# A decoder layer on one core: gate sums by distance, gates turned by transposes, the running maximum broadcast from 128 rows, and one turned output moved behind the next head's values

## The chip, the cores and the metric

The kernel runs on one core of a Trainium2 chip. A core has five engines with queues of their own. TensorE (PE in the profile; its weight loads are PEld) multiplies matrices, VectorE (DVE) and ScalarE (ACT) work element by element, GpSimd (POOL) does more of that, and SyncE (SP) issues DMAs. [...] The metric is the device time of one execution in microseconds, here the median of three runs.

## The reference

One layer of a decoder trunk for 512 positions of 1024 channels, in float32. A mixer comes first, then a feed-forward part with a short convolution; only the mixer's first group is touched by the change. It is an mLSTM with four heads of 256, worked in chunks of 128 positions:

```python
b = jnp.cumsum(lf_, axis=-1)              # lf_: log of the forget gate
dmat = jnp.where(causal, b[..., :, None] - b[..., None, :] + i_[..., None, :], -jnp.inf)
m_t = jnp.maximum(b + m[..., None], jnp.max(dmat, axis=-1))
scores = jnp.einsum("bhtd,bhsd->bhts", q_, k_) * jnp.exp(dmat - m_t[..., None])
h = num / jnp.maximum(jnp.abs(den), jnp.exp(-m_t))[..., None]
```

`num` and `den` carry a state from chunk to chunk. Each head's `h` is then normalised over its 256 channels, multiplied by a gain and by a sigmoid, and goes with the result of a convolution group (31 taps) into one output projection.

## The kernel before

**Matmuls.** The large products are made in three float32r passes: each operand is split into a high and a low part (`w_split` on ScalarE and GpSimd for weights), and `mm3` (lines 198 to 202) adds high x high, high x low and low x high. A projection of 128 columns over 512 positions (`head_proj`) is 24 such matmuls of 512 columns; a quarter of a head's values (`make_v`) is 24 matmuls of 256 columns.

**Gates.** The kernel has no state from chunk to chunk: it takes all 512 positions of a head at once. `lf` holds the logs of the forget gates, positions on the 128 partitions, four chunks by four heads as columns. `fcum` (line 613) is their running sum over all positions: for chunk `tt` a triangular matrix times `lf` of this chunk, plus a matrix of ones times `lf` of every earlier chunk, ten matmuls in float32. `ga` is input gate minus that sum. `aT` (line 621) turns `ga` to four rows of 512 by multiplying it with the identity; a scan on VectorE makes the running maximum `Mr` (line 623), `[4, 512]`. `mtok` (line 628) turns `Mr` back into positions on partitions, for `em`. `make_E(h)` (lines 593 to 604) broadcasts one row of `Mr` to 128 partitions with a float32 matmul `Mb` (line 595) whose weights are a column of the identity, repeated, and whose contraction runs over the four rows. VectorE adds the causal mask (`Md`), and ScalarE makes seven pieces of exponentials from `Md` and `Mb` into `E`.

**A head.** `attention(h)` is a generator that stops between its parts, so that the order of TensorE's work is written out by the caller. It makes the scores `s` for each chunk (line 519; VectorE multiplies them into `E`, line 520), then the outputs `o` (line 530) with their norms, then on VectorE and GpSimd a factor for each position (lines 540 to 546) and the scaled output `hn` (line 549), and at last the turned output `hT` by transposes (line 555), which VectorE reads at line 557. The loop over heads puts the next head's projections between these parts, then `make_E(h + 1)`, then `make_v(h + 1)` up to its third quarter, then the turned output of head `h`, then the fourth quarter of the values.

**Order and buffers.** TensorE's and SyncE's instructions run in the order of the program. VectorE, ScalarE and GpSimd are ordered by a planner which simulates the times and takes the ready instruction of the highest priority; the 31 taps of the convolution (line 721) have the lowest and fill VectorE. PSUM has four banks for projections (`mmbank`) and two (`atbank`) that serve `fcum`, `aT`, `mtok`, `Mb`, `s`, `o` and `hT` in turn: each takes the bank that the one before the last has left. 44 slots of `[128, 512]` in SBUF (`slot`) hold most of the intermediate tiles; `const` tiles keep their place for the whole program.

Of the kernel before, what the change touches and what calls it, by code (L numbers as in the profile page):

```python
# [10 lines left out]
F32 = mybir.dt.float32  # L11
F32R = mybir.dt.float32r
BF16 = mybir.dt.bfloat16
AF = mybir.ActivationFunctionType
ALU = mybir.AluOpType
PSUM = bass.MemoryType.PSUM

P = 128
D = 1024
T = 512  # L20
KT = D // P
NT = T // P
H = 4
# [31 lines left out]
def decoder_layer(ctx, tc, w_glu0, x, c, adaT, vecs, w_glu, w_qko, w_v0, w_v, w_out, w_up, w_down, out):  # L55
    nc = tc.nc
    V, S, G, PE = nc.vector, nc.scalar, nc.gpsimd, nc.tensor

    const = ctx.enter_context(tc.tile_pool(name="const", bufs=1))
# [28 lines left out]
    def slot(name, dt=F32):  # L88
        return slots.tile([P, T], dt, tag="t", name=name)

    def mmbank(name):
        return psum.tile([P, T], F32, tag="mm", bufs=4, name=name)

    def atbank(name):
        return psum.tile([P, T], F32, tag="at", bufs=2, name=name)
# [9 lines left out]
    ident = const.tile([P, P], F32, name="ident")  # L105
    make_identity(nc, ident)
    ones = const.tile([P, P], F32, name="ones")
    V.memset(ones, 1.0)
    tri = const.tile([P, P], F32, name="tri")
# [156 lines left out]
    for tt in range(NT):  # L266
# [9 lines left out]
        if tt < NT - 1:  # L276
# [7 lines left out]
                    op0=ALU.add)  # L284
# [140 lines left out]
    def proj(ps, pieces, off):  # L425
        for k in range(KT):
            mm3(ps, blk(pieces, off + k), u[k], k == 0, k == KT - 1)
# [46 lines left out]
    def conv4(ps, i, name):  # L474

        t = slot(f"{name}c")
        w = lambda tap: vcol("qk_conv_w", tap * 16 + i)
        S.activation(t, ps, AF.Identity, bias=vcol("qk_conv_b", i), scale=w(3))
        for d in range(1, 4):
            V.scalar_tensor_tensor(out=t[:, d:], in0=ps[:, : T - d], scalar=w(3 - d), in1=t[:, d:], op0=ALU.mult, op1=ALU.add)  # L480
        S.activation(t, t, AF.Silu)
        return t
# [11 lines left out]
    def head_proj(h, i):  # L494

        pieces, qs, ks, so = heads[h]
        ps = mmbank(f"qko{h}_{i}")
        proj(ps, pieces, i * KT)
        e = 2 * h + i % 2
        if i < 2:  # L500
            qs.append(conv4(ps, e, f"q{h}_{i}"))
        elif i < 4:
            ks.append(conv4(ps, 8 + e, f"k{h}_{i}"))
        else:
            t = slot(f"so{h}_{i}")
            S.activation(t, ps, AF.Tanh, scale=0.5)
            so.append(t)
# [3 lines left out]
    def attention(h):  # L511

        _, qs, ks, so = heads[h]

        for cc in range(NT):
            n = NS[cc]
            sp = atbank(f"s{h}_{cc}")
            for d in range(2):
                PE.matmul(sp[:, :n], ks[d][:, cc * P : (cc + 1) * P], qs[d][:, cc * P :], start=d == 0, stop=d == 1)  # L519
            V.scalar_tensor_tensor(out=E[h][cc], in0=sp[:, :n], scalar=DH**-0.5, in1=E[h][cc], op0=ALU.mult, op1=ALU.mult)  # L520
            if cc % 2:
                yield
        ssq = small.tile([P, NT], F32, tag="ssq", name=f"ssq{h}")
        dm = small.tile([P, NT], F32, tag="dm", name=f"dm{h}")
        hn = [slot(f"hn{h}_{i}") for i in range(2)]
        for tt in range(NT):
            o = atbank(f"o{h}_{tt}")
            for cc in range(tt + 1):
                a = (tt - cc) * P
                PE.matmul(o[:, : DH + 2], E[h][cc][:, a : a + P], vs[h][cc], start=cc == 0, stop=cc == tt)  # L530
            junk = small.tile([P, DH], BF16, tag="junk2", bufs=2, name=f"junko{h}_{tt}")
            hv = hn[tt // 2][:, (tt % 2) * DH : (tt % 2 + 1) * DH]
            S.activation(dm[:, tt : tt + 1], o[:, DH : DH + 1], AF.Abs)
            S.activation(hv, o[:, :DH], AF.Copy)
            S.activation(junk, hv, AF.Square, accum_out=ssq[:, tt : tt + 1])
            if tt in (1, 2):
                yield
        rd = small.tile([P, NT], F32, tag="rd", name=f"rd{h}")
        fac = small.tile([P, NT], F32, tag="fac", name=f"fac{h}")
        V.tensor_tensor(out=dm, in0=dm, in1=em[:, :, h], op=ALU.max)  # L540
        V.reciprocal(rd, dm)
        V.tensor_tensor(out=ssq, in0=ssq, in1=rd, op=ALU.mult)
        V.tensor_tensor(out=ssq, in0=ssq, in1=rd, op=ALU.mult)
        V.tensor_scalar(out=ssq, in0=ssq, scalar1=1.0 / DH, scalar2=EPS, op0=ALU.mult, op1=ALU.add)
        G.tensor_tensor(out=fac, in0=ssq, in1=mhalf, op=ALU.pow)
        V.tensor_tensor(out=fac, in0=fac, in1=rd, op=ALU.mult)
        for tt in range(NT):
            hv = hn[tt // 2][:, (tt % 2) * DH : (tt % 2 + 1) * DH]
            V.tensor_scalar(out=hv, in0=hv, scalar1=fac[:, tt : tt + 1], scalar2=None, op0=ALU.mult)
        yield  # L550
        for e in range(2):
            tp = atbank(f"hT{h}_{e}")
            for tt in range(NT):
                src = hn[tt // 2][:, (tt % 2) * DH + e * P : (tt % 2) * DH + (e + 1) * P]
                PE.transpose(tp[:, tt * P : (tt + 1) * P], src, ident)
            t = so[e]
            V.scalar_tensor_tensor(out=t, in0=t, scalar=1.0, in1=tp, op0=ALU.add, op1=ALU.mult)
            hi, lo = slot(f"hh{h}_{e}", F32R), slot(f"hl{h}_{e}", F32R)
            g = ghalf[:, 2 * h + e : 2 * h + e + 1]
            S.activation(hi, t, AF.Copy, scale=g)  # L560
            last_lo[0] = V.scalar_tensor_tensor(out=lo, in0=t, scalar=g, in1=hi.bitcast(F32), op0=ALU.mult, op1=ALU.subtract)
            hy[2 * h + e] = (hi, lo)
# [4 lines left out]
    def g16(name):  # L567
        return const.tile([P, NT, H], F32, name=name)

    fpre = gz[:, :, H : 2 * H]  # L570
    fa, fe, fu, fl, fr, lf = (g16(f"g_{i}") for i in ("fa", "fe", "fu", "fl", "fr", "lf"))
# [18 lines left out]

    E = [None] * H

    def make_E(h):
        mb = atbank(f"Mb{h}")
        PE.matmul(mb, ident[:H, h : h + 1].to_broadcast([H, P]), Mr, start=True, stop=True)
        md = slot(f"Md{h}")
        V.tensor_tensor(out=md.rearrange("p (t m) -> p t m", t=NT), in0=mb.rearrange("p (t m) -> p t m", t=NT),
                        in1=cmask[:, None, :].to_broadcast([P, NT, P]), op=ALU.add)
        E[h] = head_tiles(f"E{h}", F32)
        for cc in range(NT):  # L600
            b = ga[:, cc, h : h + 1]
            S.activation(E[h][cc][:, :P], md[:, cc * P : (cc + 1) * P], AF.Exp, bias=b, scale=-1.0)
            if cc < NT - 1:
                S.activation(E[h][cc][:, P:], mb[:, (cc + 1) * P :], AF.Exp, bias=b, scale=-1.0)
# [3 lines left out]

    fps = atbank("fcum")
    fv = fps[:, : NT * H].rearrange("p (t h) -> p t h", t=NT)  # L610
    for tt in range(NT):
        for cc in range(tt + 1):
            PE.matmul(fv[:, tt, :], tri if cc == tt else ones, lf[:, cc, :], start=cc == 0, stop=cc == tt)
    Fc, ga = g16("Fc"), g16("ga")
    V.tensor_copy(Fc, fv)
    V.tensor_tensor(out=ga, in0=gz[:, :, :H], in1=Fc, op=ALU.subtract)
    head_proj(0, 2)

    aps = atbank("aT")
    for tt in range(NT):  # L620
        PE.matmul(aps[:H, tt * P : (tt + 1) * P], ga[:, tt, :], ident, start=True, stop=True)
    Mr = const.tile([H, T], F32, name="Mr")
    V.tensor_tensor_scan(out=Mr, data0=aps[:H, :], data1=zero[:H, :].to_broadcast([H, T]), initial=0.0, op0=ALU.max, op1=ALU.max)
    head_proj(0, 3)
    mps = atbank("mtok")
    mv = mps[:, : NT * H].rearrange("p (t h) -> p t h", t=NT)
    for tt in range(NT):
        PE.matmul(mv[:, tt, :], Mr[:, tt * P : (tt + 1) * P], ident[:H, :H], start=True, stop=True)
    em = g16("em")
    V.tensor_tensor(out=em, in0=Fc, in1=mv, op=ALU.add)  # L630
    S.activation(em, em, AF.Exp, scale=-1.0)

    make_E(0)
    for i in range(4, 6):
        head_proj(0, i)


    RD = float(D) ** 0.5
# [126 lines left out]
    for h in range(H - 1):  # L765
        head_load(h + 1)
        steps = attention(h)
        if h == 0:
            head_proj(1, 0)
        next(steps)  # L770
        head_proj(h + 1, 1 if h == 0 else 0)
        next(steps)
        if h:
            head_proj(h + 1, 1)
        head_proj(h + 1, 2)
        next(steps)
        head_proj(h + 1, 3)
        next(steps)
        head_proj(h + 1, 4)
        next(steps)  # L780
        head_proj(h + 1, 5)
        make_E(h + 1)
        if h == H - 2:
            norm_mean()
        values = make_v(h + 1)
        next(values)
        for _ in steps:
            pass
        next(values)
        if h == H - 2:  # L790
            norm_sums()

# [188 lines left out]
    for i in range(NF):  # L981
# [20 lines left out]
        a = conv3(pa, i, f"fa{i}")  # L1002
# [119 lines left out]
```

## Time and profile before

| | |
|---|---|
| median of three runs | 799.61 us (798.97 to 801.39) |
| the profiled execution | 798.76 us |
| its span, first to last instruction | 796.8 us |
| TensorE's mean granted clock | 0.996 of full speed |

The profile lists for each engine what it did, and for idle time what ended it. In a row of instructions in order of time there stand the start and the duration in us, the engine, the line, the operation, the tiles written and read, and the shape; "x8" means that eight instructions are merged, and the brackets give the idle time before the first and what ended it. Durations of matmuls overlap, so the cost of one is read from the start of the next. A row of the waits has who waited for whom, the sum in us, how often, and the longest.

### The profile page before, as it was taken

What the parts mean: (1) busy time and instruction counts of PE and PEld (TensorE: products, weight loads), DVE (VectorE), ACT (ScalarE), POOL (GpSimd) and SP (SyncE); (2) the same over time, 40 slices, a digit from 0 to 9 for tenths busy, and PEclk for the clock granted to TensorE, in tenths of its full rate; (3) what the DMA queues carried; (4) which work ended last, traced back from release to release, by engine and by line L of the source; (5) the groups of instructions that cost most, each with busy time, mean ns of one, the idle gap of its engine ahead of it and who ended that gap; (6) DMA issues with size and microseconds to landing.
All of it is one profiled execution on the core that took longest, in us unless ns stands there. A gap on an engine that the chain in (4) does not pass through costs nothing.

```text
span 796.8 us, 10397 instructions
## 1 busy us (share of the span) xinstructions
PE 783.8 (98%) x3796; PEld 654.1 (82%) x3796; DVE 476.1 (60%) x748; ACT 380.0 (48%) x709; POOL 438.5 (55%) x351
## 2 busy tenths in 40 slices
PE   8999999999999999999999999999999999999996
PEld 6788897777788888888889988888888888888885
DVE  6779999999997435547958784454444453000014
ACT  6684548748474454561344454444444444222212
POOL 4799759859588443442841574444454444444420
PEclk9999999999999999999999999999999999999999
DMA  8963223123037231436854653222232222322205
GB/s 317 362 236 133 80 76 137 59 100 107 28 87 247 89 132 54 159 106 223 331 186 159 213 184 106 106 70 90 106 106 106 102 92 97 107 105 106 80 0 186
DMA packets 24887, 106.97 MB, mean 134 GB/s; under 512 B 2914, under 2 KB 2946, under 8 KB 17412
## 3 DMA queue, kind: packets, MB, share of 16 engines
q1 hardware_dynamic: 16740, 83.22, 29.2%
q10 hardware_dynamic: 8096, 23.08, 8.1%
q8 instruction: 30, 0.49, 0.2%
q14 instruction: 21, 0.17, 0.1%
HBM read 102.08 MB, written 4.21 MB: 133 GB/s over the span
## 4 chain that ended last, share of the span: by engine, by line
PE 91%; DVE 5%; ACT 2%; issue 1%; DVEq 0%; POOLq 0%; POOL 0%; ACTq 0%
PE up L201 10%; PE up L200 10%; PE up L202 10%; PE dn L202 5%; PE dn L200 5%; PE dn L201 5%; PE qko L200 4%; PE qko L201 4%; PE qko L202 4%; PE glu L348 4%; DVE cv L721 3%; PE glu L202 2%; PE glu L200 2%; PE glu L201 2%; PE s L519 2%; PE mixa L202 2%
## 5 line engine op out<-in xcount | busy, mean ns | idle before, releaser
L721 DVE SCALAR_TENSOR_TENSOR cv<-gt,cvw,cv 128x502 f32<-128x502 f32 (+24 forms) x200 | 134.7, 730 | 1.7 <-ACT cv L709 1.3
L1048 DVE TENSOR_TENSOR fo<-dn,g2r 128x512 f32<-128x512 f32 x8 | 5.5, 692 | 99.2 <-PE dn L202 99.1
L183 POOL TENSOR_TENSOR wup_1024l<-wup,wup_1024h 128x512 fp32r<-128x512 f32 x20 | 28.0, 1399 | 30.6 <-ACT wup_1024h L182 30.5
L717 POOL TENSOR_TENSOR cs<-cs,cs 128x510 f32<-128x510 f32 (+3 forms) x32 | 42.2, 1320 | 4.0 <-PE qko L202 3.4
L183 POOL TENSOR_TENSOR wup_1536l<-wup,wup_1536h 128x512 fp32r<-128x512 f32 x20 | 27.2, 1362 | 29.0 <-ACT wup_1536h L182 29.0
L183 POOL TENSOR_TENSOR wup_512l<-wup,wup_512h 128x512 fp32r<-128x512 f32 x20 | 27.7, 1386 | 23.4 <-ACT wup_512h L182 23.4
L183 POOL TENSOR_TENSOR wup_0l<-wup,wup_0h 128x512 fp32r<-128x512 f32 x20 | 26.9, 1347 | 19.5 <-ACT wup_0h L182 19.5
L201 PE MATMUL up<-u2l,wup_0h 128*128 128x512 f32 (+1 forms) x100 | 36.5, 365 | 0.2 <-DVE u2l L890 0.2
L200 PE MATMUL up<-u2h,wup_0h 128*128 128x512 f32 (+1 forms) x100 | 36.5, 365 | 0.0
L200 PE MATMUL up<-u2h,wup_1024h 128*128 128x512 f32 (+1 forms) x100 | 36.4, 364 | 0.0
L202 PE MATMUL up<-u2h,wup_0l 128*128 128x512 f32 (+1 forms) x100 | 36.4, 364 | 0.0
L202 PE MATMUL up<-u2h,wup_1536l 128*128 128x512 f32 (+1 forms) x100 | 36.4, 364 | 0.0
L200 PE MATMUL up<-u2h,wup_512h 128*128 128x512 f32 (+1 forms) x100 | 36.4, 364 | 0.0
L201 PE MATMUL up<-u2l,wup_512h 128*128 128x512 f32 (+1 forms) x100 | 36.4, 364 | 0.0
L202 PE MATMUL up<-u2h,wup_512l 128*128 128x512 f32 (+1 forms) x100 | 36.4, 364 | 0.0
L200 PE MATMUL up<-u2h,wup_1536h 128*128 128x512 f32 (+1 forms) x100 | 36.4, 364 | 0.0
L201 PE MATMUL up<-u2l,wup_1536h 128*128 128x512 f32 (+1 forms) x100 | 36.4, 364 | 0.0
L202 PE MATMUL up<-u2h,wup_1024l 128*128 128x512 f32 (+1 forms) x100 | 36.4, 364 | 0.0
L201 PE MATMUL up<-u2l,wup_1024h 128*128 128x512 f32 (+1 forms) x100 | 36.3, 363 | 0.0
L167 DVE SCALAR_TENSOR_TENSOR junk<-ada,cb 128x1024 bf16<-128x1024 f32 x20 | 32.1, 1606 | 7.0 <-DMA ada<-in_adaT 6.9
L183 POOL TENSOR_TENSOR wqko_1024l<-wqko,wqko_1024h 128x512 fp32r<-128x512 f32 x12 | 16.5, 1376 | 26.2 <-PE v L201 15.1
L183 POOL TENSOR_TENSOR wd_1024l<-wd,wd_1024h 128x512 fp32r<-128x512 f32 x11 | 14.3, 1296 | 29.8 <-ACT wd_1024h L182 29.8
(727 smaller groups left out, 2624.3 us busy)
## 6 DMA issues: line engine op xcount, KB each, us to landing
wup<-in_w_up SPq DMA_DIRECT2D x22, 1024.0 KB, 5.1
wqko<-in_w_qko SPq DMA_DIRECT2D x12, 1024.0 KB, 4.8
wd<-in_w_down SPq DMA_DIRECT2D x11, 1024.0 KB, 4.9
ada<-in_adaT ACTq DMA_DIRECT2D x20, 512.0 KB, 5.9
ada<-in_adaT SPq DMA_DIRECT2D x16, 512.0 KB, 7.6
wo<-in_w_out SPq DMA_DIRECT2D x8, 1024.0 KB, 4.7
spare<-in_adaT ACTq DMA_DIRECT2D x12, 512.0 KB, 9.2
wglu<-in_w_glu SPq DMA_DIRECT2D x5, 1024.0 KB, 7.5
```

The costliest lines, as they stand in the source:

```text
L167: t = V.scalar_tensor_tensor(out=junk, in0=r, scalar=1.0, in1=cb, op0=ALU.mult, op1=ALU.mult, accum_out=mod[:, i : i + 1])
L183: (eng or G).tensor_tensor(out=lo[:, :n], in0=src, in1=hi[:, :n].bitcast(F32), op=ALU.subtract)
L200: PE.matmul(ps, a[0], b[0], start=start, stop=False)
L201: PE.matmul(ps, a[0], b[1], start=False, stop=False)
L202: PE.matmul(ps, a[1], b[0], start=False, stop=stop)
L348: PE.matmul(ps, blk(wk, i)[a], u[k][b], start=k == 0 and p == 0, stop=k == KT - 1 and p == 1)
L519: PE.matmul(sp[:, :n], ks[d][:, cc * P : (cc + 1) * P], qs[d][:, cc * P :], start=d == 0, stop=d == 1)
L717: G.tensor_tensor(out=side[:, d:], in0=side[:, d:], in1=t[:, d:], op=ALU.add)
L721: last_tap = V.scalar_tensor_tensor(out=cp[:, d:], in0=cvx[j][:, : T - d], scalar=w(CK - 1 - d), in1=cp[:, d:], op0=ALU.mult, op1=ALU.add)
L1048: V.tensor_tensor(out=m, in0=banks[tt][hf], in1=g2r[hf], op=ALU.mult)
```

## The change

- `fcum`: one matmul for each distance between chunks, not for each pair. At distance 0 the triangular matrix multiplies all four chunks; at distance `d` the ones multiply the first `4 - d` chunks and add into the last `4 - d`.
- `aT` and `mtok` use the transpose instruction. `aT` moves behind the fourth projection of the first head, `mtok` behind its fifth, `make_E(0)` behind its sixth.
- `Mr` becomes a slot. Its high part is copied by ScalarE into rows 0 to 3 of a `[128, 512]` tile `Mhl` of float32r that GpSimd zeroes once, and VectorE puts the low part into rows 32 to 35. `pick` holds ones at the rows of each head; `Mb` is one float32r matmul over all 128 rows, which adds high and low part.
- The factor's last multiplication is gone; the instruction that scales `hn` multiplies by both numbers.
- For the first head the fourth quarter of the next head's values comes ahead of the turned output.

```diff
         G.tensor_tensor(out=fac, in0=ssq, in1=mhalf, op=ALU.pow)
-        V.tensor_tensor(out=fac, in0=fac, in1=rd, op=ALU.mult)
         for tt in range(NT):
             hv = hn[tt // 2][:, (tt % 2) * DH : (tt % 2 + 1) * DH]
-            V.tensor_scalar(out=hv, in0=hv, scalar1=fac[:, tt : tt + 1], scalar2=None, op0=ALU.mult)
+            V.tensor_scalar(out=hv, in0=hv, scalar1=fac[:, tt : tt + 1], scalar2=rd[:, tt : tt + 1], op0=ALU.mult, op1=ALU.mult)
...
+    LO = 32
+    Mhl = const.tile([P, T], F32R, name="Mhl")
+    G.memset(Mhl.bitcast(F32), 0.0)
+    pick = const.tile([P, H], F32R, name="pick")
+    G.memset(pick.bitcast(F32), 0.0)
+    for a in (0, LO):
+        G.tensor_copy(pick[a : a + H, :], ident[a : a + H, a : a + H])
+
     def make_E(h):
         mb = atbank(f"Mb{h}")
-        PE.matmul(mb, ident[:H, h : h + 1].to_broadcast([H, P]), Mr, start=True, stop=True)
+        PE.matmul(mb, pick[:, h : h + 1].to_broadcast([P, P]), Mhl, start=True, stop=True)
...
-    for tt in range(NT):
-        for cc in range(tt + 1):
-            PE.matmul(fv[:, tt, :], tri if cc == tt else ones, lf[:, cc, :], start=cc == 0, stop=cc == tt)
+    for d in range(NT):
+        PE.matmul(fv[:, d:, :], ones if d else tri, lf[:, : NT - d, :], start=d == 0, stop=d == NT - 1)
...
     head_proj(0, 2)
 
+    head_proj(0, 3)
     aps = atbank("aT")
     for tt in range(NT):
-        PE.matmul(aps[:H, tt * P : (tt + 1) * P], ga[:, tt, :], ident, start=True, stop=True)
-    Mr = const.tile([H, T], F32, name="Mr")
+        PE.transpose(aps[:H, tt * P : (tt + 1) * P], ga[:, tt, :], ident)
+    Mr = slot("Mr")[:H, :]
     V.tensor_tensor_scan(out=Mr, data0=aps[:H, :], data1=zero[:H, :].to_broadcast([H, T]), initial=0.0, op0=ALU.max, op1=ALU.max)
-    head_proj(0, 3)
+    S.activation(Mhl[:H, :], Mr, AF.Copy)
+    V.tensor_tensor(out=Mhl[LO : LO + H, :], in0=Mr, in1=Mhl[:H, :].bitcast(F32), op=ALU.subtract)
+    head_proj(0, 4)
     mps = atbank("mtok")
     mv = mps[:, : NT * H].rearrange("p (t h) -> p t h", t=NT)
     for tt in range(NT):
-        PE.matmul(mv[:, tt, :], Mr[:, tt * P : (tt + 1) * P], ident[:H, :H], start=True, stop=True)
+        PE.transpose(mv[:, tt, :], Mr[:, tt * P : (tt + 1) * P], ident[:H, :H])
...
+    head_proj(0, 5)
     make_E(0)
-    for i in range(4, 6):
-        head_proj(0, i)
...
         values = make_v(h + 1)
         next(values)
+        if h == 0:
+            next(values)
         for _ in steps:
             pass
-        next(values)
+        if h:
+            next(values)
```

## The prediction

> **What bounds the kernel now.** I read the page first, then the waits of TensorE, then TensorE's instructions in order of time around the changed lines, and last what VectorE and ScalarE do there.
>
> ```profile
> PE 783.8 (98%) x3796; PEld 654.1 (82%) x3796; DVE 476.1 (60%) x748; ACT 380.0 (48%) x709; POOL 438.5 (55%) x351
> ```
>
> ```profile
> PE cps L150 <- ACT crow L149: 3.0, 1, 3.0
> PE hT L555 <- DVE hn L549: 1.4, 1, 1.4
> PE aT L621 <- DVE ga L616: 0.7, 1, 0.7
> PE xT L244 <- ACT xr L296: 0.2, 1, 0.2
> PE up L201 <- DVE u2l L890: 0.2, 1, 0.2
> ```
>
> TensorE is busy for 98% of the span, and these five lines are all that it waited for. So a microsecond taken out of its stream is a microsecond of the kernel, unless a new wait eats it. Two of the five waits, `hT` and `aT`, stand at lines that the change touches. The other engines matter only where TensorE comes to wait for them.
>
> **The gate stage on TensorE.** Starts and durations, in order of time (a number behind x is how many instructions are merged; the next row's start tells when TensorE was free again):
>
> ```profile
> 126.96 0.28 PE L613 MATMUL fcum<-g_lf,tri 128*128 128x4 f32 x2
> ...
> 129.11 0.49 PE L200 MATMUL qko<-uh,wqko_0h 128*128 128x512 f32 x1
> ...
> 135.58 1.04 PE L621 MATMUL aT<-ident,ga 128*4 128x128 f32 x8 [0.73 <-DVE ga L616]
> 136.55 0.50 PE L200 MATMUL qko<-uh,wqko_1024h 128*128 128x512 f32 x1
> ...
> 141.67 0.39 PE L201 MATMUL qko<-ul,wqko_1536h 128*128 128x512 f32 x1
> 141.89 0.39 PE L202 MATMUL qko<-uh,wqko_1536l 128*128 128x512 f32 x1
> 142.21 1.05 PE L628 MATMUL mtok<-ident,Mr 4*128 4x4 f32 x8
> 143.12 1.10 PE L595 MATMUL Mb<-Mr,ident 4*128 4x512 f32 x2
> 144.16 0.50 PE L200 MATMUL qko<-uh,wqko_0h 128*128 128x512 f32 x1
> ...
> 144.96 0.59 PE L200 MATMUL qko<-uh,wqko_0h 128*128 128x512 f32 x1
> ...
> 148.33 0.43 PE L202 MATMUL qko<-uh,wqko_0l 128*128 128x512 f32 x1
> ```
>
> Each float32 matmul here is two instructions, and a projection's float32r matmul of 512 columns is one, started 0.23 us after the one before it (141.67 to 141.89).
>
> 1. *Sums by distance.* Ten matmuls (20 instructions) take 129.11 - 126.96 = 2.15 us, 0.108 us an instruction. Four (8 instructions) remain. They are up to 16 columns wide instead of 4; the nearest row with wider columns is `aT`, 0.97 us / 8 = 0.121 us at 128 columns. So they take 0.86 to 0.97 us, and I take 0.86, as 16 is nearer to 4. **Gain 1.29 us** (1.18 to 1.29).
>
> 2. *The wait for `ga`.* TensorE stood 0.73 us at 135.58. The third projection is now followed by the fourth, 24 steps of 0.23 = 5.5 us, before the turn. **Gain 0.73 us**, covered by that projection; without that cover the wait is back. What is late next is the scan, which now has to end before `mtok`, with only the fifth projection between:
>
> ```profile
> 138.86 1.21 DVE L623 TENSOR_TENSOR_SCAN Mr<-aT,zero 4x512 f32<-4x512 f32 x1
> ```
>
> It started 2.3 us after `aT` left TensorE and took 1.21: 3.5 us against 5.5. Behind it VectorE gets one subtraction of 4x512 and ScalarE one copy of 4x512, needed only at the end of the sixth projection, another 5.5 us on. Nothing on TensorE waits for them, so I cost them at nothing.
>
> 3. *Transposes in place of matmuls.* Eight instructions become four at `aT` (0.97 us) and at `mtok` (144.16 - 143.12 is `Mb`; 143.12 - 142.21 = 0.91). What a transpose costs is seen at the turned outputs of the heads, which are transposes already; here the second head's, which did not wait, and the first head's, which did:
>
> ```profile
> 208.02 0.28 PE L202 MATMUL v<-wv_5h,ul 128*128 128x256 f32 x1
> 209.74 1.46 PE L555 MATMUL hT<-ident,hn 128*128 128x128 f32 x8 [1.45 <-DVE hn L549]
> 210.96 0.36 PE L200 MATMUL v<-wv_0h,uh 128*128 128x256 f32 x1
> ...
> 265.28 1.04 PE L555 MATMUL hT<-ident,hn 128*128 128x128 f32 x8
> 266.07 0.36 PE L200 MATMUL v<-wv_0h,uh 128*128 128x256 f32 x1
> ```
>
> ```profile
> L555 PE MATMUL hT<-ident,hn 128*128 128x128 f32 x32 | 4.6, 278 | 1.4 <-DVE hn L549 1.4
> ```
>
> Eight take 266.07 - 265.28 = 0.79 us, one instruction each, so four take 0.40; with 0.12 apiece as in `aT`, 0.48. I take 0.47 and 0.46. **Gain 0.5 + 0.45 us**. [...]
>
> 4. *The maximum's broadcast `Mb`, once for each head.* It is two instructions of float32 from 4 rows, now one of float32r from 128 rows.
>
> ```profile
> 198.36 1.12 PE L595 MATMUL Mb<-Mr,ident 4*128 4x512 f32 x2
> 199.41 0.39 PE L200 MATMUL v<-wv_0h,uh 128*128 128x256 f32 x1
> ```
>
> It costs 1.05 us for the second head and 144.16 - 143.12 = 1.04 for the first. One float32r step is 0.23; one half of the old pair would be 0.52. I take 0.25, since the projections run exactly this form. **Gain 4 x 0.8 = 3.2 us** (2.1 to 3.3). The zeroing of the 128-row tile and of `pick` falls to GpSimd, which the page shows at 55% and whose work no wait of TensorE names; nothing feeds them but constants. I cost them at nothing.
>
> 5. *The granted clock.* Right after `mtok` and `Mb` the projection's steps are twice as far apart: from 144.96 to 148.33 eight steps take 3.37 us, 0.42 each. The windows view (busy time, instructions, granted clock) says why:
>
> ```profile
> 146.00:148.00 2.00, 2.00 (x6) 0.50 0.00 0
> ```
>
> At 0.23 these eight would take 1.84, so 1.5 us were lost. What stands ahead of it is 142.12 to 144.16, 2.04 us in which the array sees matmuls with 4 rows only. `aT`'s stretch with its wait, about 1.7 us, has no such sequel. After the change no stretch of this stage is longer than 0.5 us, a projection stands between any two, and `Mb` fills all 128 rows. **Gain 1.5 us** in this execution. [...]
>
> 6. *Behind the next head's values.* Between the values' matmul at 208.02 and the next at 210.96 lie 2.94 us; 0.12 is an ordinary step and 0.79 the eight transposes, so the wait with its ragged end costs 2.03 us. Now 24 more steps of 0.12 (2.9 us) come ahead of the turn. VectorE's side:
>
> ```profile
> 207.90 0.16 DVE L546 TENSOR_TENSOR fac<-fac,rd 128x4 f32<-128x4 f32 x1
> 207.98 1.36 DVE L721 SCALAR_TENSOR_TENSOR cv<-gt,cvw,cv 128x495 f32<-128x495 f32 x2
> 209.25 1.14 DVE L549 TENSOR_SCALAR hn<-hn,fac 128x256 f32<-128x256 f32 x4
> 210.30 1.37 DVE L721 SCALAR_TENSOR_TENSOR cv<-gt,cvw,cv 128x494 f32<-128x494 f32 x2
> 211.57 0.69 DVE L557 SCALAR_TENSOR_TENSOR so<-so,hT 128x512 f32<-128x512 f32 x1
> ```
>
> `hn` was ready at 210.30, 2.16 us after TensorE was free. TensorE now comes 2.9 later, less 0.8 for its shorter `Mb`; and `fac`'s multiplication with the two taps behind it (1.35 us) is gone from the chain. So `hn` is there some 1.3 us early, and the 2.03 go. What is late next: the second head's scores now follow the turn at once, and their bank is that of the first turned half. It comes free only when L557 has read it. Until now the last part of the values, 2.9 us, stood between. The wait is L557's start after the first four transposes, plus its 0.69, less the 0.40 that the other four take. With VectorE free and 0.1 for the hand-over it is 0.4 us. Behind the two taps that stood ahead of L557 here (1.27) it is 1.6. VectorE works taps without a break in this stage, so I take one tap, 1.0 us. **Net gain 1.0 us** (0.4 to 1.6). The dropped multiplication itself costs TensorE nothing either way in the other heads, whose `hT` does not wait.
>
> 7. *`Mb` of the first head behind the sixth projection.* The second of the scores' banks is the one that `Mb` leaves. Between them lie now only the next head's first projection and the first scores:
>
> ```profile
> 162.24 1.02 PE L519 MATMUL s<-q_0c,k_2c 128*128 128x512 f32 x2
> ...
> 163.96 0.49 PE L519 MATMUL s<-q_0c,k_2c 128*128 128x384 f32 x1
> ```
>
> ```profile
> 151.71 0.40 ACT L602 ACTIVATE E<-Md,ga 128x128 f32<-128x128 f32 x1
> ...
> 204.79 0.40 ACT L602 ACTIVATE E<-Md,ga 128x128 f32<-128x128 f32 x1
> ```
>
> That is 5.5 + 1.72 = 7.2 us. The last exponential that reads `Mb` ended 7.95 us after TensorE left it for the first head (152.11 - 144.16), and 5.78 for the second (205.19 - 199.41). So the wait is 0 to 0.8 us. VectorE no longer has the keys' convolutions at this place, which is nearer the second head's case: I take 0.
>
> Everything behind these places moves as it is, because loads and splits follow TensorE's progress.
>
> **Sum.** 1.29 + 0.73 + 0.5 + 0.45 + 3.2 + 1.5 + 1.0 = 8.7 us. The profiled execution took 798.76 us, so 790.1; the median of the runs, 799.61, is 0.85 above it, so **790.9 us**.
>
> **Rivals.**
> *B: the clock's share does not show.* Either the drop stood in the profiled execution alone (the three runs spread over 2.4 us, more than its 1.5), or it returns at the turn of the first head, where the transposes (0.79) and the scores' wait (1.0 to 1.6) make up to 2.4 us in which TensorE does no matmul. Against it: after the change that stretch is shorter than the present one at 208.14 to 210.96. Time 790.9 + 1.5 = 792.4 us; with the long wait as well, 793.0.
> *C: the exponentials of the first head come late.* The present 7.95 us for it, against 5.78 one head later, speak for it. It gives 791.7 us as it stands; if ScalarE's new order also puts five splits of weights (0.63 each, the row under D) ahead, 3.1 us more, 794.8.
> *D, on the other side: weights behind saturated transfers.* In the output projection's second half ScalarE waits for weights:
>
> ```profile
> 392.96 0.63 ACT L182 ACTIVATE wo_0h<-wo 128x512 fp32r<-128x512 f32 x1 [6.66 <-DMA wo<-in_w_out]
> ```
>
> ```profile
> 393.67 2.10 POOL L183 TENSOR_TENSOR wo_0l<-wo,wo_0h 128x512 fp32r<-128x512 f32 x1 [1.41 <-ACT wo_0h L182]
> ```
>
> ```profile
> 401.99 0.47 PE L200 MATMUL mixb<-wo_0h,yh 128*128 128x512 f32 x1
> ```
>
> The remaining weights are first read at 401.99, 6.2 us after that split. The planner orders ScalarE's queue anew, and it issues the loads that compete. If the transfer stays where it is while TensorE arrives 8.7 us earlier, TensorE waits 2.5 us: 793.4. To be slower than before by 0.3% it would have to land 6.2 + 8.7 + 2.4 = 17.3 us later: 802 us. Against it: those loads are released by TensorE's own progress.
> *E: the transposes don't overlap.* Each then takes its own 278 ns, four 1.1 us at `aT` and at `mtok`, where 0.97 and 0.91 stand now: 0.95 us of gain become 0.3 of loss, 792.2 us. The eight in 0.79 speak against it. [...]
>
> **How the numbers follow.** Chances: the forecast 0.58, B 0.22, C 0.09, E 0.04, D (and other effects of a new order on the queues) 0.07. The range begins at the sum with the best ends (8.7 + 0.1 + 0.6 = 9.4, so 790.2), less the 0.64 us by which the fastest run lies under the median: 789.5. It ends beyond B and the middle of C, at 795.5. About 0.3%, 2.4 us, is what can be told from no change here. Faster needs under 797.2: all but D and the far end of C, 0.89; within 0.05; slower 0.06.
>
> **What would show it.** Right: TensorE's waits list neither `aT` nor `hT`; eight instructions for `fcum`, four each for `aT` and `mtok`, one `Mb` a head in about 0.23 us; no stretch at clock 0.5 near 145; a short wait of the scores for L557 near 205. Wrong: a wait of over 2 us at these scores, at the first head's scores for an exponential, or at `mixb` for weights; or `Mb` at 0.5 us.

## The result, and the profile after

The changed kernel is slower. Its median is 805.76 us (805.36 to 806.8, six runs), against 799.29 us (797.27 to 801.39, six runs) of the kernel before beside it: 6.5 us more, a ratio of 1.0083, interval 1.0066 to 1.0099. The forecast was 790.9 us with a range of 789.5 to 795.5. The profiled execution took 805.77 us, its span 804.1 us, 7.3 us above that of before.

The page's first row and TensorE's waits (who waited for whom, the sum in us, how often, the longest):

```profile
PE 783.0 (97%) x3772; PEld 654.6 (81%) x3772; DVE 481.4 (60%) x745; ACT 380.6 (47%) x710; POOL 435.2 (54%) x355
```

```profile
PE hT L554 <- DVE hn L548: 5.5, 5, 1.9
PE cps L150 <- ACT crow L149: 3.1, 1, 3.1
PE hT L554 <- ACT E L611: 2.4, 1, 2.4
PE s L519 <- DVE so L556: 1.8, 1, 1.8
```

`aT` is gone from the list, as forecast. `hT`, which had 1.4 us, now stands there twice, with 5.5 and 2.4 us. One could believe that the gate stage's parts failed. They did not; this is TensorE there, in order of time:

```profile
127.12 0.29 PE L619 MATMUL fcum<-g_lf,tri 128*128 128x16 f32 x2
...
127.93 0.49 PE L200 MATMUL qko<-uh,wqko_0h 128*128 128x512 f32 x1
...
138.96 0.60 PE L628 MATMUL aT<-ident,ga 128*4 128x128 f32 x4
139.31 0.48 PE L200 MATMUL qko<-uh,wqko_0h 128*128 128x512 f32 x1
...
144.96 0.41 PE L637 MATMUL mtok<-ident,Mr 4*128 4x4 f32 x4
145.29 0.50 PE L200 MATMUL qko<-uh,wqko_1024h 128*128 128x512 f32 x1
145.63 0.39 PE L201 MATMUL qko<-ul,wqko_1024h 128*128 128x512 f32 x1
...
150.87 0.40 PE L602 MATMUL Mb<-Mhl,pick 128*128 128x512 f32 x1
151.10 0.39 PE L200 MATMUL qko<-uh,wqko_0h 128*128 128x512 f32 x1
```

From each step to the next row's start: the sums take 0.81 us, `aT` 0.35, `mtok` 0.33, `Mb` 0.23, none waits, and behind `mtok` the projection goes on in steps of 0.23 to 0.34, so the clock does not drop there. The first scores start at 156.57 us, 5.67 earlier than before. Where TensorE stands against before, place by place (start of the same instruction in both traces):

| place on TensorE | before | after | difference |
|---|---|---|---|
| gate sums `fcum` | 126.96 | 127.12 | +0.16 |
| first head's first scores | 162.24 | 156.57 | -5.67 |
| second head's first values | 199.41 | 192.83 | -6.58 |
| second head's second pair of scores | 222.41 | 224.78 | +2.37 |
| third head's broadcast `Mb` | 255.50 | 257.77 | +2.27 |
| third head's first scores | 269.02 | 277.27 | +8.25 |
| fourth head's turned output `hT` | 362.84 | 370.06 | +7.22 |

Everything is lost at two places, where the first and where the second head's output is turned: 8.95 us at the first (from -6.58 to +2.37) and 6.9 at the second, where TensorE arrives at 266.63, 1.35 us later than before since the third `Mb` is shorter, and leaves 8.25 us later. Behind the third turn the difference stays as it is.

**The first turn**, all engines in order of time:

```profile
199.90 5.21 DVE L729 SCALAR_TENSOR_TENSOR cv<-gt,cvw,cv 128x495 f32<-128x495 f32 x8
...
201.17 1.05 POOL L545 TENSOR_TENSOR fac<-ssq,mhalf 128x4 f32<-128x4 f32 x1
...
204.22 0.28 PE L202 MATMUL v<-wv_5h,ul 128*128 128x256 f32 x1
...
204.80 1.27 POOL L183 TENSOR_TENSOR wqko_1024l<-wqko,wqko_1024h 128x512 fp32r<-128x512 f32 x1
...
205.03 5.00 DVE L548 TENSOR_SCALAR hn<-hn,fac,rd 128x256 f32<-128x256 f32 x4
...
206.36 0.30 PE L554 MATMUL hT<-ident,hn 128*128 128x128 f32 x1 [1.87 <-DVE hn L548]
...
210.08 1.33 PE L554 MATMUL hT<-ident,hn 128*128 128x128 f32 x5 [0.92 <-DVE hn L548]
212.50 1.27 DVE L556 SCALAR_TENSOR_TENSOR so<-so,hT 128x512 f32<-128x512 f32 x2
...
213.23 2.08 PE L519 MATMUL s<-q_0c,k_2c 128*128 128x512 f32 x2 [1.82 <-DVE so L556]
...
218.80 0.90 PE L200 MATMUL qko<-uh,wqko_0h 128*128 128x512 f32 x1
```

TensorE is free at 204.34 (204.22 and a step of 0.12). The factor is ready at 202.22, but VectorE begins to scale `hn` only at 205.03, behind eight taps, and takes 5.00 us for what took 1.14. The scores start at 213.23 instead of the 205.13 that eight transposes (0.79) would need: 8.1 us. They then take 218.80 - 213.23 = 5.57 us instead of 2.72 (213.91 to 216.63 before), with the clock at half. With the 2.03 us of wait that before had, 8.1 + 2.85 - 2.03 = 8.9. The clock, in windows of 4 us (busy time and instructions of TensorE, granted clock, DMA share, GB/s):

```profile
208.00:212.00 4.00, 1.68 (x6) 0.63 0.38 137
212.00:216.00 4.00, 2.77 (x4) 0.50 0.00 0
...
272.00:276.00 4.00, 4.00 (x21) 0.50 0.01 2
```

The clock is already down (0.63) in the window from 208 to 212, in which six of the eight scattered transposes stand; no run here separates them from idle time. The granted clock is 0.50 from 209.0 to 219.2 us, and at the second turn from 270.4 to 277.2.

**The second turn**, all engines:

```profile
260.32 2.10 DVE L167 SCALAR_TENSOR_TENSOR junk<-ada,cb 128x1024 bf16<-128x1024 f32 x1
...
263.70 1.22 DVE L167 SCALAR_TENSOR_TENSOR junk<-ada,cb 128x1024 bf16<-128x1024 f32 x1
...
266.16 2.33 DVE L548 TENSOR_SCALAR hn<-hn,fac,rd 128x256 f32<-128x256 f32 x4 [0.83 <-POOL fac L545]
...
268.41 0.67 DVE L604 TENSOR_TENSOR Md<-Mb,cmask 128x512 f32<-128x512 f32 x1
...
269.12 0.40 ACT L609 ACTIVATE E<-Md,ga 128x128 f32<-128x128 f32 x1 [1.37 <-DVE Md L604]
...
271.24 1.11 PE L554 MATMUL hT<-ident,hn 128*128 128x128 f32 x4 [2.37 <-ACT E L611]
```

Sums that belong to the conditioning (L167, eight of them in all, each with a load of its own) stand between the links of this head's chain on VectorE. The program puts them behind the last tap, which starts at 237.5 us here and at 229.4 before. `hn` starts at 266.16; in the kernel before the last of the eight sums was ahead of the chain, and `hn` started at 259.95, with TensorE at 265.28:

```profile
255.19 1.23 DVE L167 SCALAR_TENSOR_TENSOR junk<-ada,cb 128x1024 bf16<-128x1024 f32 x1 [1.59 <-DMA ada<-in_adaT]
...
259.95 2.14 DVE L549 TENSOR_SCALAR hn<-hn,fac 128x256 f32<-128x256 f32 x4
```

In the changed kernel `Md` stands behind `hn`, the exponentials behind `Md`, and the second half of `hT` takes the bank that `Mb` leaves only after the last exponential. TensorE goes on with values at 272.01, and at half clock it needs 5.26 us for what took 2.95.

Both turns have VectorE in common. Its busy time by stage, in the kernel before and then after (stage and its length; then PE, PEld, DVE, ACT and POOL, each with its instructions):

```profile
112.00:160.00 48.00, 47.27 (x233) 38.79 (x232) 47.69 (x80) 37.24 (x65) 41.70 (x33) 0.96 0.27 96
160.00:205.00 45.00, 45.00 (x215) 36.57 (x214) 43.61 (x72) 28.67 (x62) 35.43 (x29) 1.00 0.24 86
```

```profile
112.00:160.00 48.00, 48.00 (x232) 39.25 (x231) 47.63 (x79) 37.56 (x67) 43.65 (x35) 1.00 0.29 99
160.00:205.00 45.00, 44.49 (x244) 38.77 (x242) 44.84 (x74) 32.08 (x68) 34.02 (x28) 1.00 0.23 82
```

The page gives VectorE 60% of the span. In the 93 us ahead of the first turn it was busy for 91.3 us before (98%) and for 92.5 after (99%). And the taps that stand ahead of the first `hn`, by the windows that end there (window, length, VectorE's busy time and number of taps), before and then after:

```profile
0.00:209.25 209.25, 121.41 (x181) 0.99 0.43 153
```

```profile
0.00:205.03 205.03, 117.04 (x175) 1.00 0.43 156
```

Six taps fewer, 4.4 us of VectorE's time, and `hn` starts 4.2 us earlier. It did not follow TensorE's 6.58; it came when VectorE had worked off what stands ahead of it.

### The profile page after: what moved, and what is told of

The parts are those of the page before. It is cut to its first block, busy times and chain, and to the rows that moved or that the text cites. A ratio compares the mean times of both kernels' runs of the same rounds, so it can differ in the third digit from the quotient of the medians.

```text
span 804.1 us, 10347 instructions
## 1 busy us (share of the span) xinstructions
PE 783.0 (97%) x3772; PEld 654.6 (81%) x3772; DVE 481.4 (60%) x745; ACT 380.6 (47%) x710; POOL 435.2 (54%) x355
## 4 chain that ended last, share of the span: by engine, by line
PE 79%; DVE 12%; DMA 3%; issue 2%; ACT 2%; POOL 2%; SPq 0%; DVEq 0%; POOLq 0%; ACTq 0%
PE up L201 10%; PE up L202 10%; PE up L200 10%; DVE cv L729 6%; PE dn L200 5%; PE dn L202 5%; PE dn L201 5%; PE qko L200 2%; PE qko L202 2%; PE qko L201 2%; PE glu L201 2%; PE glu L202 2%; PE glu L200 2%; PE s L519 2%; PE mixa L200 2%
## 5 line engine op out<-in xcount | busy, mean ns | idle before, releaser
L729 DVE SCALAR_TENSOR_TENSOR cv<-gt,cvw,cv 128x502 f32<-128x502 f32 (+23 forms) x200 | 134.2, 727 | 1.7 <-ACT cv L717 1.3
L167 DVE SCALAR_TENSOR_TENSOR junk<-ada,cb 128x1024 bf16<-128x1024 f32 x20 | 31.8, 1592 | 5.4 <-DMA ada<-in_adaT 5.3
```

What stands on the lines that cost most here:

```text
L167: t = V.scalar_tensor_tensor(out=junk, in0=r, scalar=1.0, in1=cb, op0=ALU.mult, op1=ALU.mult, accum_out=mod[:, i : i + 1])
L729: last_tap = V.scalar_tensor_tensor(out=cp[:, d:], in0=cvx[j][:, : T - d], scalar=w(CK - 1 - d), in1=cp[:, d:], op0=ALU.mult, op1=ALU.add)
```

## Experiments

Three explanations stood at first: (1) the move lets GpSimd's weight splits start earlier, and they collide with the scaling of `hn`; (2) the scaling by two numbers is itself slow; (3) VectorE is full, runs in a fixed order, and is late as a whole. Later runs ask whether a relief of VectorE brings the forecast gain back.

**The move undone in the changed kernel.**

```diff
         next(values)
-        if h == 0:
-            next(values)
         for _ in steps:
             pass
-        if h:
-            next(values)
+        next(values)
```

> The changed kernel with the first head's turned output again ahead of the fourth quarter of the next head's values. Theory 1 (collision): the early quarter frees the values' weight buffers, GpSimd's splits of the next weights start sooner and run beside the four scalings hn of the first head, which take 1.25 us each for 0.3. Undone: the four in about 1.2 us, hT waits 1.5 us at most, no clock 0.5 near 210, and all of the gate stage's gain is left: 799.3 - 5.8 (gate stage up to the first scores) - 2.4 (three further Mb) = 791 to 793 us. Theory 2 (the scaling by two numbers is itself slow): four scalings still 5 us, 800 us or more. Theory 3 (the planner's new order of VectorE, whatever stands where): still over 798 us.

803.92 us (10 runs), ratio 1.0053 (1.0035 to 1.007). VectorE of this run at the turn, in order of time, and TensorE's wait:

```profile
204.44 5.21 DVE L729 SCALAR_TENSOR_TENSOR cv<-gt,cvw,cv 128x495 f32<-128x495 f32 x8
209.57 1.37 DVE L548 TENSOR_SCALAR hn<-hn,fac,rd 128x256 f32<-128x256 f32 x4
```

```profile
PE hT L554 <- DVE hn L548: 5.9, 2, 5.0
```

The four scalings take 1.37 us: without the move GpSimd is idle there (from 209.29 to 214.14) and nothing collides. Yet TensorE waits 5.0 us at this turn, behind the same eight taps, and 2.4 us for the exponentials at the second. From the second head's first values (196.36) to its second pair of scores (224.07) TensorE loses 4.7 us against the kernel before, where the changed kernel lost 8.95; at the second turn it loses 5.7 us, where that lost 6.9. So the move and the collision with it are worth some 4 us at the first turn, and the rest stands without them.

The medians are only 1.8 us apart. In the profiled execution TensorE reached `fcum` 3.14 us later than in the kernel before, with 1.9 us of waits in the stage ahead of it (`glu`), which the change does not touch; from `fcum` to the end it lost 2.2 us, the changed kernel 7.0. Whether the other executions have this too is not known.

**The factor's multiplication back in the changed kernel**, scaling by one number:

```diff
         G.tensor_tensor(out=fac, in0=ssq, in1=mhalf, op=ALU.pow)
+        V.tensor_tensor(out=fac, in0=fac, in1=rd, op=ALU.mult)
...
-            V.tensor_scalar(out=hv, in0=hv, scalar1=fac[:, tt : tt + 1], scalar2=rd[:, tt : tt + 1], op0=ALU.mult, op1=ALU.mult)
+            V.tensor_scalar(out=hv, in0=hv, scalar1=fac[:, tt : tt + 1], scalar2=None, op0=ALU.mult)
```

> The changed kernel with the factor's last multiplication back and the scaling by one number; the values' fourth quarter stays ahead. Theory 1: hn's four still about 5 us, 803 to 808 us. Theory 2: hn's four 1.2 us, 790 to 794 us. Theory 3: anything else.

805.27 us (4 runs), ratio 1.0077 (1.0047 to 1.0106): as slow as the changed kernel, with 7.7 us of waits for `hn`. The second explanation falls. The four scalings started 4.1 us later, in part behind the product and two more taps, and took 3.17 us instead of 5.00:

```profile
209.11 3.17 DVE L549 TENSOR_SCALAR hn<-hn,fac 128x256 f32<-128x256 f32 x4
```

The two that ran beside GpSimd took 1.37 and 1.35 us; the other two, behind GpSimd's last split, took 0.34 each. So the form with one number pays beside GpSimd as well.

**The move alone, in the kernel before.**

```diff
         next(values)
+        if h == 0:
+            next(values)
         for _ in steps:
             pass
-        next(values)
+        if h:
+            next(values)
```

> The kernel before with only the values' fourth quarter moved ahead of the first head's turned output. Theory 1: hn's four 4 to 5 us beside GpSimd's splits, a wait of hT and of the second head's scores, clock 0.5 after it; 805 to 813 us. Theory 2 and 3 (the move is harmless, the scaling's form or the gate part's new order does it): 797 to 800 us.

799.02 us (10 runs), ratio 1.0 (0.9984 to 1.0017). VectorE at the turn, and what TensorE then waits for:

```profile
210.36 1.14 DVE L549 TENSOR_SCALAR hn<-hn,fac 128x256 f32<-128x256 f32 x4
211.41 2.63 DVE L721 SCALAR_TENSOR_TENSOR cv<-gt,cvw,cv 128x494 f32<-128x494 f32 x4
```

```profile
PE s L519 <- DVE so L557: 1.5, 1, 1.5
```

The wait of `hT` is gone, and the scores wait 1.5 us instead, behind four taps. In the order of the kernel before, the move by itself neither harms nor helps. It does not price the collision: GpSimd's split starts at 210.76 here, 0.4 us behind the first scaling, and it is the split that takes longer (1.89 us), while the four scalings keep their 1.14.

**The first head's scaling on ScalarE**, in the changed kernel with the factor's multiplication back:

```diff
+            if h == 0:
+                S.activation(hv, hv, AF.Copy, scale=fac[:, tt : tt + 1])
+            else:
+                V.tensor_scalar(out=hv, in0=hv, scalar1=fac[:, tt : tt + 1], scalar2=None, op0=ALU.mult)
```

> The changed kernel with the factor's multiplication back, and for the first head alone the four scalings hn made by ScalarE, which does nothing between 205 and 212 us. Theory 1: 0.4 us each, ready before the turn, hT waits under 0.5 us, only the scores' wait for L557's kind of reading is left (0.5 to 1.8 us); 790 to 794 us. Theory 3 (VectorE's queue as a whole is late, taps ahead of everything): the factor and the reading of hT are as late as now, 797 us or more.

802.2 us (10 runs), ratio 1.0036 (1.0015 to 1.0058). The collision is out of the way, and the median is 3.6 us below the changed kernel's, though the ten executions run from 798.25 to 804.3. In the profiled one the first turn costs 5.6 us instead of 8.95. But TensorE still waits 2.3 us for `hn`, since the factor itself comes only behind eight taps, then 1.4 us for `so` behind six more, and 2.4 us at the second turn. What is left is VectorE's queue.

**What a scaling costs beside GpSimd**, a kernel of its own: four VectorE instructions of 128x256, alone and beside six subtractions on GpSimd.

```diff
+            for _ in range(beside):
+                G.tensor_tensor(out=big, in0=src, in1=other, op=ALU.subtract)
+            V.tensor_copy(mark, gm)
+            for i in range(4):
+                one(form, d[:, i * 256 : (i + 1) * 256], i)
```

> A kernel of its own, which computes nothing of the layer: five forms of VectorE instructions on 128x256, four of each, first with GpSimd idle and then beside six subtractions of 128x512 on GpSimd from SBUF to SBUF (1.3 us each): scaling by one number, scaling by two, scaling by two with a sum written out, a convolution tap with its sum in PSUM, a product of two SBUF tiles. If the 1.25 us of each hn in the changed kernel is a collision with GpSimd: the first two 0.3 to 0.45 us alone and 1.2 to 1.4 beside; the tap the same in both. If the scaling by two numbers is slow by itself: the second over 1 us alone too.

Its groups by line and shape (busy us, mean ns of one; idle time before):

```profile
L45 DVE TENSOR_SCALAR ts_beside<-ts_beside,col 128x256 f32<-128x256 f32 x4 | 5.3, 1379 | 0.0
...
L49 DVE SCALAR_TENSOR_TENSOR bank<-tap_beside,col,bank 128x256 f32<-128x256 f32 x4 | 1.9, 487 | 0.1
L49 DVE SCALAR_TENSOR_TENSOR bank<-tap_alone,col,bank 128x256 f32<-128x256 f32 x4 | 1.9, 487 | 0.1
...
L45 DVE TENSOR_SCALAR ts_alone<-ts_alone,col 128x256 f32<-128x256 f32 x4 | 1.4, 408 | 0.0
```

Scaling by two numbers takes 408 ns alone and 1379 ns beside GpSimd, about one GpSimd instruction (1.27 us) each. The four of the changed kernel, 5.00 us, are this case. By one number it takes 347 ns alone; the mean of the group meant to run beside GpSimd is 604, but there GpSimd began late, behind a load:

```profile
5.86 2.16 DVE L43 TENSOR_SCALAR ts_beside<-ts_beside,col 128x256 f32<-128x256 f32 x4
...
6.61 7.96 POOL L61 TENSOR_TENSOR big<-x,x 128x512 f32<-128x512 f32 x6 [0.85 <-DMA x<-in_x]
```

Three of these four started before it and took 0.34 to 0.35 us, the one beside it 1.37. So both forms pay alike. The form of a tap, which adds in PSUM, takes 487 ns either way, so the taps hide that GpSimd is there at all. Why the one form is slowed and the other is not, no run here shows.

Why GpSimd worked there after the change and not before is seen in its first row behind the turn, in the kernel before:

```profile
212.54 1.30 POOL L183 TENSOR_TENSOR wqko_1024l<-wqko,wqko_1024h 128x512 fp32r<-128x512 f32 x1 [7.26 <-PE v L201]
```

The split waited for the values' last quarter, which stood behind the turn. With the quarter ahead of it, the split starts at 204.80, beside `hn`.

**Fewer taps**, five less for each channel block (40 in all; the convolution's result lacks them), in the kernel before and in the changed one:

```diff
-        for d in range(SIDE + 1, CK):
+        for d in range(SIDE + 1, CK - 5):
```

> The kernel before with five of the convolution's 25 taps on VectorE left out for each of the eight channel blocks (40 taps, about 26 us of VectorE's work; the convolution's result lacks them). It is the base for the next run. Theory A (VectorE's full queue is what the first two heads' turns wait for) and theory B (the changed parts cost time by themselves) both expect the wait of hT to go: 796 to 799 us.

> The changed kernel with the same 40 taps left out. Theory A: with room in VectorE's queue hn is ready for both heads, hT waits under 1 us in all, no clock 0.5 after 200 us, and the gate stage's 5.8 us and the three further Mb's 2.4 us show: 6 to 9 us below the previous run, 788 to 792 us. Theory B (collision by the move, slower scaling): still some microseconds above the previous run, 800 us or more.

806.02 us (ratio 1.0093, 1.007 to 1.0117) and 808.15 us (1.0121, 1.0096 to 1.0146), 4 runs each. The first is above what was expected. The second lies by its number where the collision had it, but not by its cause, as the first head's four scalings took 2.35 us there. The planner put other work into the time that became free. In the changed kernel without these taps VectorE has conditioning sums, several of them waiting for their loads, ahead of the reading of `hT`; the scores wait 9.6 us for that reading, and `fcum` waits 4.8 us. In the kernel before without them `fcum` waits 2.9 us and the scores 2.8 in all. So this pair says nothing on the amount of work: it came with another order, and the order was worse. The next runs leave the work as it is and write the order out.

**Taps behind the turns**, in the changed kernel: the last two channel blocks of the convolution come behind the first and second head's turned output, the conditioning sums behind the second head's `hn`.

```diff
+    for j in range(6):
+        conv_block(j)
...
+        if h < 2:
+            tc.cur_priority += LATER
+            conv_block(KT - 2 + h, last_lo[0])
+            tc.cur_priority -= LATER
...
-        ada_block(i, last_tap)
+        ada_block(i, hn_of[1])
```

> The changed kernel, nothing left out, with VectorE's order relieved: the taps of channel block 6 behind the first head's turned output, those of block 7 behind the second head's, the eight sums of the conditioning rows behind the second head's scaling. 150 taps stand ahead of the first hn (175 in the changed kernel). Theory A: hT waits under 1 us, the scores for L556's reading 0.5 to 1 us; 790 to 793 us. Theory B: GpSimd's splits still collide with hn and the second head still waits; 798 us or more.

796.53 us (6 runs), ratio 0.9977 (0.9957 to 0.9997), between the two expected ranges.

```profile
194.24 3.33 DVE L550 TENSOR_SCALAR hn<-hn,fac,rd 128x256 f32<-128x256 f32 x4 [1.23 <-POOL fac L547]
```

150 taps instead of 175 stand ahead of the first `hn`, and no `hT` waits. At the second turn TensorE is 8.28 us ahead of the kernel before: the gain exists. Then it goes again, 2.1 us at the third head's first scores, which wait behind four sums, and more behind them; 3.46 us are left at the end.

**The same without the move.**

```diff
-        if h == 0:
-            next(values)
         for _ in steps:
             pass
-        if h:
-            next(values)
+        next(values)
```

> As the previous run, with the first head's turned output ahead of the fourth quarter of the values again. Theory A: hn comes just in time or up to 2 us late, the scores don't wait; 790 to 793 us, within 1.5 us of the previous run. If the move is what matters: over 3 us from it.

797.76 us (10 runs), ratio 0.9981 (0.9969 to 0.9994): above the expected range, but, as expected, not to be told from the run above. At the second turn TensorE is 7.63 us ahead; the third head's scores then wait 4.7 us behind five sums.

**The sums behind the second turn, or behind the last tap**: the run with taps behind the turns, and in it only the sums' place changed.

```diff
-        ada_block(i, hn_of[1])
+        ada_block(i, lo_of[1])
```

> The run with taps behind the turns, with the eight sums of the conditioning rows behind the second head's turned output too (four of them stood ahead of its reading, for which the scores waited 1.9 us). VectorE's order as the bound: that wait goes, about 2 us below that run's 796.5: 793 to 796 us. If the waits only move to the next place: 796 to 798.

803.73 us (4 runs), ratio 1.0054 (1.0035 to 1.0072), above both expected ranges. The wait behind sums is gone but for 0.3 us, TensorE is 8.01 us ahead at these scores, and then it waits 8.4 us for `ysum`, the convolution's last block, whose taps now end late among the sums.

```diff
-        ada_block(i, hn_of[1])
+        ada_block(i, last_tap[0])
```

> As the previous run, with the eight sums behind the last tap as in the changed kernel, so after block 7's taps. They then fall between 285 and 305 us, where VectorE has room ahead of the third head's scaling. 793 to 796 us; if they hold up the third head's scaling, 797 or more with a wait of hT near 310.

**793.18 us** (792.92 to 793.6, 4 runs), ratio 0.9921 (0.9904 to 0.9939): 6.1 us faster than the kernel before and 12.6 below the changed kernel. TensorE's longest waits, and VectorE ahead of and at the first turn:

```profile
PE cps L150 <- ACT crow L149: 2.9, 1, 2.9
PE ry_s L208 <- DVE so L559: 1.9, 1, 1.9
...
```

```profile
193.78 3.33 DVE L550 TENSOR_SCALAR hn<-hn,fac,rd 128x256 f32<-128x256 f32 x4 [1.23 <-POOL fac L547]
...
206.15 1.28 DVE L559 SCALAR_TENSOR_TENSOR so<-so,hT 128x512 f32<-128x512 f32 x2 [7.83 <-PE hT L557]
```

The scaling of `hn` starts 11.7 us ahead of its use (205.52); the collision is still there (3.33 us) and costs nothing. VectorE waits 7.83 us for TensorE, no longer the other way round. TensorE is 8.94 us ahead of the kernel before at the third turn; 3.8 us go again in the fourth head: 1.9 in the wait of `ry_s` behind two of the sums, 1.4 in the scores after it (319.28 to 323.46 instead of 2.79 us, with the clock at 0.74 from 320 to 324), and the rest was not followed.

**The same relief in the kernel before**, with the sums as in the first of these runs.

> The kernel before with the same relief of VectorE's order as in the run with taps behind the turns (blocks 6 and 7 behind the first and the second head's turns, the sums behind the second head's scaling). If TensorE's work is the bound there and only hT's 1.4 us waits for VectorE: 796 to 799 us, and the changed parts then are worth the difference to the relieved changed kernel, up to 7 us at the second head's turn. If the relief by itself is the gain and the change's parts are worth nothing: the same as the relieved changed kernel, 794 to 796.5.

803.54 us (4 runs), ratio 1.0052 (1.0037 to 1.0067), above both expected ranges. At the second turn TensorE is where it was in the kernel before (+0.07); the third head's scores then wait 3.0 us behind five sums. So this relief alone is no gain. With it the changed parts are worth 803.54 - 796.53 = 7.0 us in the medians (6.0 by the two ratios), and 8.35 at the second turn (-8.28 against +0.07), or 7.6 if both are counted from `fcum`, which the profiled executions reached 0.44 and 1.21 us later than before.

The kernel before with the sums behind the last tap, the order of the fastest run, was not run. How much of that run's 6.1 us the order alone would have brought is therefore not shown.

## Why the prediction was wrong

- *Sums by distance* (1.29 foretold): 2.15 - 0.81 = 1.34. Right, just above its range (1.18 to 1.29).
- *The wait for `ga`* (0.73): gone. Right.
- *Transposes* (0.5 and 0.45): 0.97 - 0.35 = 0.62 and 0.91 - 0.33 = 0.58. Right, a little cheaper than taken; rival E falls with it.
- *`Mb`* (0.8 a head): 1.04 - 0.23 = 0.81. Right.
- *The clock behind `mtok`* (1.5): no drop there in this execution. Right, and the drop was not a matter of one execution, as rival B had it. Each of the four traces with the old gate stage has the clock at 0.50 for 3.4 us in it: behind `mtok` and `Mb` the kernel before (from 145.0 us), fewer taps (149.6) and the relief (147.7), behind the sums the move alone (131.8), fewer taps (132.5) and the relief (130.6). Of the nine traces with the new stage one has a drop there, the run with fewer taps, at its 4.8 us wait of `fcum`. What decides between the two places is not shown. TensorE reached the first scores 5.83 us earlier than `fcum` let expect, where the parts up to there summed to 5.27.
- *Exponentials of the first head* (no wait): none. Rival C fell here; the same mechanism came at the second turn instead (2.37 us), behind VectorE.
- *Behind the next head's values* (net 1.0) is the step that failed, in its words "`hn` is there some 1.3 us early". It counted the chain from the head's last output to `hn` 1.35 us shorter, because an instruction and two taps went out of it. By that, with the last output's start 5.67 us earlier, `hn` would start at about 202.2 and be done at 203.3. It started at 205.03, 2.8 us later, and took 5.00 us instead of 1.14, 3.9 longer. The first part is VectorE's queue: the factor was ready at 202.22, and the two taps that were to go out of the chain stood in it all the same, now among the eight ahead of `hn`. The chain became longer, not shorter (18.2 us from the last output to `hn` before, 19.7 after, 20.7 with the move undone), because what stands between its links is a fixed list of taps that VectorE, 99% busy, works off at its own rate. The second part is the collision, which the prediction priced at nothing, as it took the duration from a stage in which GpSimd was idle. The trace of the kernel before shows it one head later, where the four took 2.14 us: the one beside GpSimd 1.35, the others 0.34 or 0.35 each. The short wait for `so` (1.0 foretold) was 1.8.
- Behind it stands the sentence "Everything behind these places moves as it is, because loads and splits follow TensorE's progress". The split behind the values' last quarter does (204.80 instead of 212.54). VectorE's list does not: at the first turn TensorE came 6.58 us earlier and `hn` 4.2, and the lead became waits of 1.87, 0.88, 0.94 and 0.92 us for `hn`. The prediction had the reason before it ("VectorE works taps without a break in this stage") and used it only for the single wait behind `so`.
- The waits then cost more than themselves. Rival B had the clock come back at this turn at a price of 1.5 us; it did, and again at the second turn, for 2.85 and 2.3 us, behind stretches without matmuls but transposes of 8.9 us (204.34 to 213.23) and 5.4 us (266.63 to 272.01) against that rival's 2.4. So the change lost more than it had gained.
- Rival D held its 0.07 for "other effects of a new order on the queues". That is the nearest to what happened; its own mechanism, weights at `mixb`, did not show. No rival named VectorE as the bound. Of the signs of being wrong none came as named (the scores waited 1.8 us, not over 2); what failed was the sign of being right that `hT` leaves the list of waits.

With the order on VectorE written out, the sum holds: up to the second turn the parts make 5.27 + 2 x 0.8 + 1.0 = 7.9 us. There the first relieved run was 8.28 us ahead of the kernel before and the fastest 7.92; counted from `fcum`, 8.7 and 9.3. The relief in the kernel before is 1.1 us ahead by the same count, so some 7.6 and 8.1 us are the changed parts'.

What stays open: how exactly the 8.95 us of the first turn divide. Without the move 4.7 us are left and with the scaling on ScalarE 5.6, so the collision is worth some 3.4 to 4.3 us, but both runs also changed the order. Why the planner leaves eight taps between two links of that chain was not tried. That a lighter VectorE in the same order would have been enough was not shown either, since the runs with fewer taps came with another order.

## What to carry to other kernels

Before a gain on the busiest engine is booked, look at the busy time of the others by stage, not over the span: an engine at 60% overall was at 99% where it mattered, and it did not come earlier because its consumer did (`hn` 4.2 us, by six taps fewer, where TensorE came 6.58 earlier). At each place where they meet, count what stands in the full engine's queue ahead of the wanted instruction, and write filler work behind that place explicitly; the place of eight sums alone was worth 10.5 us (803.73 against 793.18). And when a transfer or a matmul is moved ahead, ask which buffer it frees and which engine then starts to work beside the critical instruction.

## What the hardware showed that was not expected

A scaling of 128x256 from SBUF to SBUF by two numbers took 408 ns alone and 1379 ns beside GpSimd, and by one number about 350 and 1370, while a tap with its sum in PSUM took 487 ns in both cases. And where TensorE waited for 8.1 and 4.6 us, with only transposes in between, its clock fell to half, for 10.2 and 6.8 us: three and two times the 3.4 us of the drop in the kernel before. That doubled the next scores (5.57 us instead of 2.72) and nearly doubled the next values (5.26 instead of 2.95).
